# The first layer norm of a hybrid decoder block: ScalarE normalises, scale and bias move to the transposed tiles, and the residual is finished during the up-projection

## The chip, the cores and the metric

One core of a Trainium2 chip runs the whole block as one program. Its engines have queues of their own: TensorE (PE in the profile; PEld is its weight load), VectorE (DVE), ScalarE (ACT), GpSimd (POOL), and SyncE (SP), whose queue here issues all the DMAs that matter. The metric is the device time of one execution in microseconds (us), the median of several.

## The reference, cut to what matters

One layer, 1024 tokens, width 1024, all float32. The change touches the first norm, and what reads its result: the up-projection, and the residual of the second norm.

```python
mixed = (jax.nn.sigmoid(gate_a) * y_a + jax.nn.sigmoid(gate_b) * y_b) @ w_out[i]
x = layer_norm(DEEPNORM_ALPHA * x + mixed, ln1_g[i], ln1_b[i])
h = causal_dwconv(x @ w_up[i], conv_w[i], conv_b[i])          # 1024 -> 5632, 3 taps
h_gate, h_val = jnp.split(h, 2, axis=-1)
ffn = (jax.nn.silu(h_gate) * h_val) @ w_down[i]
x = layer_norm(DEEPNORM_ALPHA * x + ffn, ln2_g[i], ln2_b[i])
...
def layer_norm(x, g, b):                                      # over the last axis
    return (x - mu) * rsqrt(var + 1e-5) * g + b
```

## The kernel before

**Precision.** Each float32 operand of a product is split into a high and a low part in the matmul's own format (`wh`/`wl` for weights): ACT writes the high part (L101), DVE or POOL subtracts it from the source to give the low part (L103, L106). A product is three matmuls, high times high, high times low, low times high (`mm3`, L155).

**Stages.** Input projection, scores and selection, the two token mixers and their projections run until about 1171 us. Then, on which the change bears:

- The out-projection with the first norm, about 1171 to 1302 us (`tm_phase`, L890, called with `FOURS`). The 8 token tiles t = 0 to 7 of 128 tokens go in two groups of four; each group runs over 4 blocks of 256 columns of `w_out`. After each block DVE adds the PSUM to the scaled residual `res` (L965, `mixed`) and takes statistics (L910). When a group's last block is through, `fin1(t)` (L946) follows for each of its tiles, that of group 1 among the matmuls of group 2, that of group 2 (tiles 4 to 7) with no out-projection left behind it. Here this last stretch is called the tail.
- `fin1` runs `layer_norm` (L873), 8 transposes of 128x128 on PE (L88), the copy of the PSUM into `xq` on ACT (L958) and, after each second tile, `x_sets` (L932), which makes the right-hand operands of the up-projection, `XS[0..6]`, by sums on DVE and POOL (L164) and splits (L101, L106). Then SP stores `res` to `d_x1[t]` in HBM (L961).
- `layer_norm`: BN_AGGR on DVE (L876), rsqrt as two small POOL operations (L212, L213), then two DVE passes over 128x1024 (L884: subtract the mean, times the gain; L887: times rsqrt, plus the bias). The gain and bias lie in `gb`, each loaded broadcast to all partitions. Tiles 1 and 3 (`SPREAD`) go another way: one small DVE operation (L879), ACT normalises (L880), DVE multiplies (L881), POOL adds (L882).
- The up-projection, 22 steps f = 0 to 21, about 1294 to 1735 us (`up(f)`, L1006). A step has 7 products p0 to p6 of 12 matmuls with 512 columns (a Winograd-like scheme), 84 matmuls. Its weights come as two raw tiles (`wr` in even steps, `ar` in odd ones) by SP (L995); `left_operands` makes seven weight sets from them by sums on DVE (L164), high parts on ACT, low parts on POOL (DVE in part for f = 0). This chain, DVE, ACT, POOL and again DVE, is called the ring below. DVE gathers the products into `h` (L1020), `conv` runs on ACT (L1062) and DVE (two passes, L1064), ACT makes the silu, POOL the product, and SP stores to `d_act` (L1074).
- The down-projection reads `d_act` back, with `w_down` in `dr` tiles, and `d_x1` as the residual of the second norm (L1183).

**Buffers.** Seven weight sets have seven slots (`wq` 4, `fp` 3): one step's worth. The tag `dr` of pool `raws` holds one buffer at a time. The `ch` PSUM tiles have 8 banks, four in use by a step.

**What sets the order.** The kernel is built with a scheduler that plays a model of the time at build, and writes each engine's queue by it. The place of a line in the code is therefore not its place in the queue; on an engine, instructions run strictly in the order of the queue. Orders shown below are those queues.

## Time and profile before

| | us |
|---|---|
| median of 3 executions (lowest, highest) | 2160.23 (2158.56, 2161.76) |
| the profiled execution | 2157.95 |
| its span in the trace | 2156.2 |
| PE busy in it | 2067.9 |
| DVE busy in it | 1585.9 |

The span runs from the first to the last instruction of the trace, and the remaining 1.75 us lie around it. A row of a timeline has the start, the duration, the engine, the line, the operation, its output and input and the count; a bracket at its end is the idle time of the engine just before it and what ended that. The mean granted TensorE clock is 0.983 of full speed.

### The profile page before, as it was taken

The page shows a single profiled execution, that of the slowest core. Times are in us where ns is not written, and L with a number is a line of the kernel's source. Part 1 is how long each engine was busy: PE and PEld are TensorE (multiplying, and loading weights), DVE is VectorE, ACT ScalarE, POOL GpSimd, SP SyncE. Part 2 cuts the span into 40 slices and gives each one's busy share as a digit, 9 for nine tenths or more (in the row PEclk, how much of TensorE's full clock was granted, in tenths as well). Part 3 has the DMA queues.
Part 4 walks back from the last instruction along what each step waited for, and adds up shares of the span by engine and source line. Part 5 has one row for each costly group of instructions (what it writes and reads, how often), then busy time and mean ns, then how long its engine had stood idle before and what let it go on. Part 6 is the DMA issues. An engine that isn't in the chain of part 4 may idle for free.

```text
span 2156.2 us, 32472 instructions
## 1 busy us (share of the span) xinstructions
PE 2067.9 (96%) x12210; PEld 1815.2 (84%) x12210; DVE 1585.9 (74%) x2700; ACT 841.9 (39%) x1498; POOL 996.8 (46%) x808
## 2 busy tenths in 40 slices
PE   9999999999999999999999979999999978989997
PEld 8888899998988888887788977877777768989897
DVE  3489999999227888786234587777777789986965
ACT  4343312213126766675222244434443444332421
POOL 2432443634431121213332676767767765444743
PEclk9999999999999999999999989999999989999999
DMA  4222211211226776779666351222222134223222
GB/s 137 79 64 79 86 33 55 62 45 52 74 77 126 140 153 133 141 160 227 209 198 148 129 173 49 88 79 78 79 79 88 55 124 150 89 93 118 89 98 79
DMA packets 377566, 227.14 MB, mean 105 GB/s; under 512 B 189328, under 2 KB 351760, under 8 KB 377408
## 3 DMA queue, kind: packets, MB, share of 16 engines
q1 hardware_dynamic: 377408, 225.06, 38.3%
q8 instruction: 96, 1.57, 0.3%
q14 instruction: 62, 0.51, 0.1%
HBM read 146.37 MB, written 40.89 MB: 87 GB/s over the span
## 4 chain that ended last, share of the span: by engine, by line
PE 22%; DVE 12%; POOL 8%; issue 7%; DMA 2%; ACT 2%; SPq 0%; POOLq 0%; DVEq 0%; ACTq 0%
PE mm L155 12%; PE ch L155 10%; POOL wl L106 5%; DVE au L106 2%; DVE cv L1064 1%; DVE wu L106 1%; DVE um L164 1%; DVE h L1020 1%; DVE dr L164 1%; DMA wr<-d_ob 1%; DVE ar L164 1%; ACT cv L1062 1%; DVE res_all L164 1%; POOL lnmv L212 1%; DMA dr<-in_w_down_dram 1%
## 5 line engine op out<-in xcount | busy, mean ns | idle before, releaser
L106 POOL TENSOR_TENSOR wl<-wr,wh 128x512 fp32r<-128x512 f32 x304 | 439.9, 1460 | 287.3 <-ACT wh L101 279.7
L155 PE MATMUL ch<-xs,wh 128*128 128x512 f32 x1232 | 384.8, 394 | 6.7 <-ACT wh L101 4.1
L155 PE MATMUL mm<-Ah,wh 128*128 128x512 f32 x832 | 331.6, 399 | 2.2 <-ACT wh L101 1.3
L155 PE MATMUL mm<-Al,wh 128*128 128x512 f32 x832 | 330.1, 397 | 0.3 <-POOL Al L106 0.3
L155 PE MATMUL mm<-Ah,wl 128*128 128x512 f32 x832 | 329.3, 396 | 0.0
L155 PEld LDWEIGHTS ch<-xs,wh 128*128 128x128 f32 x1232 | 231.7, 189 | 59.4 <-ACT wh L101 4.6
L103 POOL TENSOR_SCALAR wh<-wr 128x512 fp32r<-128x512 f32 x112 | 76.9, 690 | 383.2 <-PE mm L155 199.8
L155 PE MATMUL ch<-xs,wl 128*128 128x512 f32 x616 | 242.4, 394 | 6.6 <-POOL wl L106 6.5
L155 PE MATMUL ch<-wu,au 128*128 128x256 f32 x1512 | 197.1, 294 | 31.2 <-DVE um L164 14.4
L155 PEld LDWEIGHTS ch<-wu,au 128*128 128x128 f32 x1512 | 192.5, 201 | 36.0 <-DVE um L164 14.7
L155 PE MATMUL mm<-wl,Ah 128*128 128x256 f32 x768 | 217.8, 285 | 4.7 <-POOL wl L106 4.6
L155 PE MATMUL mm<-wh,Al 128*128 128x256 f32 x768 | 216.3, 284 | 0.0
L155 PE MATMUL mm<-wh,Ah 128*128 128x256 f32 x768 | 213.8, 284 | 0.0
L1064 DVE SCALAR_TENSOR_TENSOR cv<-h,cw,cv 128x1023 f32<-128x1023 f32 x88 | 167.6, 1905 | 59.9 <-ACT cv L1062 58.4
L101 ACT ACTIVATE wh<-wr 128x512 fp32r<-128x512 f32 (+1 forms) x201 | 120.6, 622 | 186.7 <-PE mm L155 77.0
L155 PEld LDWEIGHTS mm<-Ah,wh 128*128 128x128 f32 x832 | 156.3, 188 | 32.9 <-ACT wh L101 1.8
L155 PEld LDWEIGHTS mm<-Ah,wl 128*128 128x128 f32 x832 | 156.2, 188 | 32.9
L155 PEld LDWEIGHTS mm<-Al,wh 128*128 128x128 f32 x832 | 156.4, 188 | 30.5 <-POOL Al L106 0.8
L651 DVE MATCH_REPLACE8 score<-m,score 128x896 f32<-128x896 f32 (+3 forms) x192 | 166.4, 868 | 0.0
L650 DVE MAX8 m<-score 128x8 f32<-128x896 f32 (+3 forms) x192 | 163.4, 875 | 2.3 <-POOL score L457 2.1
L155 PEld LDWEIGHTS mm<-wl,Ah 128*128 128x128 f32 x768 | 145.8, 190 | 6.4 <-POOL wl L106 5.7
L106 POOL TENSOR_TENSOR wl<-ar,wh 128x512 fp32r<-128x512 f32 x77 | 127.7, 1677 | 44.9 <-ACT wh L101 44.9
(261 smaller groups left out, 4327.0 us busy)
## 6 DMA issues: line engine op xcount, KB each, us to landing
wr<-in_w_in_dram SPq DMA_DIRECT2D x60, 512.0 KB, 3.9
wr<-in_w_up_dram SPq DMA_DIRECT2D x22, 512.0 KB, 3.9
ar<-in_w_up_dram SPq DMA_DIRECT2D x22, 512.0 KB, 3.9
d_act<-cv SPq DMA_DIRECT2D x22, 512.0 KB, 2.6
dr<-in_w_down_dram SPq DMA_DIRECT2D x12, 768.0 KB, 7.1
ar<-d_act SPq DMA_DIRECT2D x12, 768.0 KB, 5.7
d_tg<-tg SPq DMA_DIRECT2D x32, 256.0 KB, 2.0
wr<-in_w_out_dram SPq DMA_DIRECT2D x16, 512.0 KB, 3.6
```

What stands on the lines that cost most here:

```text
L101: S.activation(dst, src, AF.Copy, scale=scale)
L103: (V if eng == "V" else G).tensor_scalar(dst, src, scale, 0.0, ALU.mult, ALU.add)
L106: done["GV"[eng != "G"]] = (G if eng == "G" else V).tensor_tensor(out=dst, in0=src, in1=hi.bitcast(F32), op=ALU.subtract)
L155: T.matmul(ps, lhsT=l, rhs=r, start=start, stop=stop, skip_group_check=more)
L164: (G if eng == "G" else V).tensor_tensor(out=out, in0=a, in1=b, op=op)
L212: G.tensor_scalar(dst, src, scale, eps, ALU.mult, ALU.add)
L650: V.max(m8, score[t])
L651: V.match_replace(score[t], m8, score[t], TAKEN)
L1020: V.tensor_tensor(out=out, in0=a, in1=quad(b), op=ALU.add)
L1062: S.activation(o, h, AF.Identity, bias=cbias[:, c:c + 1], scale=cw[:, 2, c:c + 1])
L1064: V.scalar_tensor_tensor(o[:, d:], h[:, :L - d], cw[:, 2 - d, c:c + 1], o[:, d:], ALU.mult, ALU.add)
```

## The change

`plain_norm` replaces `layer_norm` in `fin1`: ACT normalises each tile in two halves of 512 columns without gain and bias, with a small DVE operation (L877 of the changed kernel) for its bias pointer. Gain and bias are applied after the transposes, where they lie along the partitions: each of the 8 transposed pieces of 128x128 of a tile is read out of PSUM with its own scale and bias column, four by ACT (L974) and four by DVE (L972), in place of two ACT copies of 128x512. The columns come by two small loads into `gb1`. The broadcast loads of gain and bias leave the out-projection. The rows stored are those without gain and bias, to a new `d_n1` (L977). `finish_x1(t)` loads them again into the one buffer `X1`, multiplies by the gain and adds the bias on DVE (two operations of 128x1024, L164 with the name `x1w`), and stores `d_x1` (L1102); it is called after steps f = 4 to 11. `X1` has the tag `dr`, so `w_down`'s first load comes after it. The `SPREAD` path goes. The seven weight slots are dealt differently: sets 0 and 5 lie in an early pool, 1 to 4 in `wq`, 6 in `fp`.

```diff
--- before.py
+++ after.py
@@ -249,6 +249,7 @@
     d_oa = [dp.tile([P, L], F32, name=f"d_oa{j}") for j in range(8)]
     d_ob = [dp.tile([P, L], F32, name=f"d_ob{j}") for j in range(8)]
     d_x1 = [dp.tile([P, D], F32, name=f"d_x1{t}") for t in range(NT)]
+    d_n1 = [dp.tile([P, D], F32, name=f"d_n1{t}") for t in range(NT)]
     d_act = [dp.tile([P, 6, L], F32, name=f"d_act{c}") for c in range(4)]
     d_ma = [dp.tile([P, L], F32, name=f"d_ma{j}") for j in range(8)]
 
@@ -867,8 +868,16 @@
             nc.sync.dma_start(cw[:, i], conv_w[0, i].rearrange("(f p) -> p f", p=P))
         nc.sync.dma_start(cbias, conv_b[0].rearrange("(f p) -> p f", p=P))
 
-    def load_gb(pl, g, b):
-        return [bcast_row(pl, vec[0], D, nm("gb")) for vec in (g, b)]
+    def plain_norm(t, nseg, eps):
+
+        r = RS["res"][t]
+        mv = RS["pool"].tile([P, 4], F32, name=nm("lnmv"), tag="lnmv", bufs=2)
+        V.bn_aggr(mv[:, 0:2], RS["stats"][t][:, :nseg])
+        rsqrt_of(mv[:, 2:3], mv[:, 1:2], 1.0, eps, 1)
+        V.scalar_tensor_tensor(mv[:, 3:4], mv[:, 0:1], -1.0, mv[:, 2:3], ALU.mult, ALU.mult)
+        for h in range(2):
+            c = slice(h * HALF, (h + 1) * HALF)
+            S.activation(r[:, c], r[:, c], AF.Identity, bias=mv[:, 3:4], scale=mv[:, 2:3])
 
     def layer_norm(t, nseg, gb, eps, spread=False, cuts=1):
         r = RS["res"][t]
@@ -922,12 +931,15 @@
     segx = ExitStack()
     segd, segk = ExitStack(), ExitStack()
     xpool = pool("xset", stack=segx)
+    fp0 = pool("ffearly", stack=segx)
+    gb1 = fp0.tile([P, 2, KT], F32, name="gb1")
+    for i, v in enumerate((ln1_g, ln1_b)):
+        nc.sync.dma_start(gb1[:, i], v[0].rearrange("(k p) -> p k", p=P))
     open_residual([x[t * P:(t + 1) * P, :] for t in range(NT)], 5)
     XS = [bpool.tile([P, 2, 4, HALF], F32R, name=nm("xs"), tag="B") for _ in range(4)]
     with ExitStack() as c1:
         lp = pool("ln1", stack=c1)
-        gb1 = load_gb(lp, ln1_g, ln1_b)
-        SPREAD, XE, XA = (1, 3), ('GVGVGVG', 'GVGVGVG', 'GGGVGGG', 'VVGVVGV'), ('VVVV', 'VVVV', 'VVVV', 'VVVG')
+        XE, XA = ('GVGVGVG', 'GVGVGVG', 'GGGVGGG', 'VVGVVGV'), ('VVVV', 'VVVV', 'VVVV', 'VVVG')
 
         def x_sets(i, xf):
 
@@ -944,9 +956,8 @@
         xfs = {}
 
         def fin1(t, nseg):
-            layer_norm(t, nseg, gb1, EPS, t in SPREAD)
+            plain_norm(t, nseg, EPS)
             r = RS["res"][t]
-            tap(f"x1_{t}", r)
             xf = xfs.setdefault(t // 2, [])
             for g in range(2):
                 pt = bank("mm" if t >= 4 else "pt", (P, 4, P))
@@ -955,10 +966,15 @@
                 for k in range(4):
                     n = g * 4 + k
                     turn_tile(pt[:, k], r[:, n * P:(n + 1) * P])
-                S.activation(quad(xq), pt, AF.Copy)
+                for k in range(4):
+                    n, c = g * 4 + k, slice(k * P, (k + 1) * P)
+                    if k % 2:
+                        V.tensor_scalar(xq[:, c], pt[:, k], gb1[:, 0, n:n + 1], gb1[:, 1, n:n + 1], ALU.mult, ALU.add)
+                    else:
+                        S.activation(xq[:, c], pt[:, k], AF.Identity, bias=gb1[:, 1, n:n + 1], scale=gb1[:, 0, n:n + 1])
             if t % 2:
                 x_sets(t // 2, xf)
-            nc.sync.dma_start(d_x1[t], r)
+            nc.sync.dma_start(d_n1[t], r)
 
         def mixed(ps, rvs, *_):
             for j, rv in enumerate(rvs):
@@ -997,7 +1013,7 @@
             for _ in range(7):
                 n = nset[0] % 7
                 nset[0] += 1
-                pl, nb = (wq, 4) if n < 4 else (fp, 3)
+                pl, nb = ((fp0, 2), (wq, 4), (wq, 4), (wq, 4), (wq, 4), (fp0, 2), (fp, 1))[n]
                 W.append([pl.tile([P, 512], F32R, name=nm(x), tag=x, bufs=nb) for x in ("wh", "wl")])
             run(left_operands(raw[1][:, :512], raw[1][:, 512:], raw[0][:, :512], raw[0][:, 512:],
                               lambda j, src: split(*W[j], src, "A", (UE if f else UE0)[j]), US))
@@ -1074,11 +1090,24 @@
                 nc.sync.dma_start(d_act[f // 6][:, f % 6], out_[0])
             return p0, p1, p5, p2, p3, p4, conv1, p6, conv0
 
+        X1 = rawp.tile([P, 3, D], F32, name="x1w", tag="dr")
+
+        def finish_x1(t):
+            nc.sync.dma_start(X1[:, 0], d_n1[t])
+            if t == 0:
+                for i, v in enumerate((ln1_g, ln1_b)):
+                    nc.sync.dma_start(X1[:, 1 + i], v[0].unsqueeze(0).to_broadcast([P, D]))
+            for i, op in enumerate((ALU.mult, ALU.add)):
+                sums(X1[:, 0], X1[:, 0], X1[:, 1 + i], op)
+            nc.sync.dma_start(d_x1[t], X1[:, 0])
+
         late = []
         for f in range(NF):
             p0, p1, p5, p2, p3, p4, conv1, *rest = up(f)
             run([p0, p1, *late[:1], p5, *late[1:], p2, p3, p4, conv1])
             late = rest
+            if 4 <= f < 4 + NT:
+                finish_x1(f - 4)
         late[0]()
         last_conv = late[1]
     segx.close()
```

What the built queues hold, at three places. First DVE in the tail, where the last out-projection blocks of tiles 4 to 7 end (`res` the residual tiles, `mm` PSUM, `lnmv` mean and variance, `wl`/`wh`/`wr` weights of step 0). Before:

```order
L965 SCALAR_TENSOR_TENSOR res_12260<-res_12260,mm_12824 128x256
L876 BN_AGGR lnmv_12905<-stats_12254 128x2
L910 BN_STATS stats_12255<-res_12260 128x6
L884 SCALAR_TENSOR_TENSOR res_12258<-res_12258,lnmv_12905,gb_11734 128x1024
L876 BN_AGGR lnmv_12926<-stats_12255 128x2
L965 SCALAR_TENSOR_TENSOR res_12262<-res_12262,mm_12851 128x256
L887 SCALAR_TENSOR_TENSOR res_12258<-res_12258,lnmv_12905,gb_11736 128x1024
L884 SCALAR_TENSOR_TENSOR res_12260<-res_12260,lnmv_12926,gb_11734 128x1024
L106 TENSOR_TENSOR wl_13047<-wr_13044,wh_13046 128x512
```

After:

```order
L981 SCALAR_TENSOR_TENSOR res_12268<-res_12268,mm_12831 128x256
L919 BN_STATS stats_12264<-res_12268 128x6
L106 TENSOR_TENSOR wl_13110<-wr_13107,wh_13109 128x512
L981 SCALAR_TENSOR_TENSOR res_12270<-res_12270,mm_12858 128x256
L875 BN_AGGR lnmv_12939<-stats_12264 128x2
L164 TENSOR_TENSOR wr_13107<-wr_13107,wr_13105 128x512
L919 BN_STATS stats_12265<-res_12270 128x6
L981 SCALAR_TENSOR_TENSOR res_12272<-res_12272,mm_12885 128x256
```

The low part `wl` of a first weight set, and a sum of its raw weights, moved from behind the first three passes of the norm to either side of tile 5's residual; the norm's passes are gone from this queue.

Second, DVE around the end of `x_sets` and step 0 of the up-projection (`xs` the operands that p0 to p6 read, `h` the gathered products). Before:

```order
L106 TENSOR_TENSOR xs_11730<-xq_12993,xs_11730 128x4x128
L164 TENSOR_TENSOR wr_13042<-wr_13042,wr_13044 128x512
L106 TENSOR_TENSOR xs_11728<-xq_13000,xs_11728 128x4x128
L164 TENSOR_TENSOR wr_13044<-wr_13044,wr_13042 128x512
L106 TENSOR_TENSOR wl_13049<-wr_13042,wh_13048 128x512
L106 TENSOR_TENSOR wl_13053<-wr_13044,wh_13052 128x512
L106 TENSOR_TENSOR wl_13059<-wr_13044,wh_13058 128x512
L1020 TENSOR_TENSOR h_13091<-h_13092,ch_13094 128x4x128
L164 TENSOR_TENSOR ar_13168<-ar_13168,ar_13166 128x512
L164 TENSOR_TENSOR ar_13166<-ar_13166 128x512
L164 TENSOR_TENSOR ar_13166<-ar_13166,ar_13168 128x512
L1020 TENSOR_TENSOR h_13092<-h_13092,ch_13094 128x4x128
```

After:

```order
L164 TENSOR_TENSOR x1w<-x1w 128x1024
L164 TENSOR_TENSOR xq_13059<-xq_13059,xq_13021 128x512
L106 TENSOR_TENSOR xs_11744<-xq_13049,xs_11744 128x4x128
L106 TENSOR_TENSOR xs_11742<-xq_13059,xs_11742 128x4x128
L164 TENSOR_TENSOR ar_13231<-ar_13231,ar_13229 128x512
L164 TENSOR_TENSOR ar_13229<-ar_13229 128x512
L1036 TENSOR_TENSOR h_13154<-h_13155,ch_13157 128x4x128
L164 TENSOR_TENSOR x1w<-x1w 128x1024 x2
L164 TENSOR_TENSOR ar_13229<-ar_13229,ar_13231 128x512
L164 TENSOR_TENSOR x1w<-x1w 128x1024
L1036 TENSOR_TENSOR h_13155<-h_13155,ch_13157 128x4x128
L164 TENSOR_TENSOR x1w<-x1w 128x1024
```

The last `xs` operation now stands behind four `x1w` operations (rows of tiles 0 and 1, the last of them shown first here); weight low parts that followed it have gone ahead; and tiles 2 and 3 stand among step 0's gathers. The remaining `x1w` operations follow in steps 1 to 3, two for each tile.

Third, SP from the loads of step 1's weights on (`d_n` the rows without gain and bias, `d_x` the finished ones, their numbers one per tile). Before:

```order
L961 DMA d_x_141<-res_12258 128x1024
L995 DMA ar_13168<-in_w_up_dram 128x8x128
L995 DMA ar_13454<-in_w_up_dram 128x8x128
L1117 DMA dr_16222<-in_w_down_dram 128x6x256 x2
L961 DMA d_x_142<-res_12260 128x1024
L961 DMA d_x_143<-res_12262 128x1024
L961 DMA d_x_144<-res_12264 128x1024
L995 DMA wr_13310<-in_w_up_dram 128x8x128
```

After:

```order
L977 DMA d_n_149<-res_12268 128x1024
L1096 DMA x1w<-d_n_145 128x1024
L1099 DMA x1w<-in_ln_g_dram 128x1024
L1099 DMA x1w<-in_ln_b_dram 128x1024
L977 DMA d_n_150<-res_12270 128x1024
L1011 DMA wr_13373<-in_w_up_dram 128x8x128
L977 DMA d_n_151<-res_12272 128x1024
L977 DMA d_n_152<-res_12274 128x1024
L1102 DMA d_x_137<-x1w 128x1024
L1096 DMA x1w<-d_n_146 128x1024
L1011 DMA wr_13375<-in_w_up_dram 128x8x128
L1102 DMA d_x_138<-x1w 128x1024
```

The store of each tile's rows is followed by reloads into `x1w` one after another, each behind the store of the tile ahead of it; `w_down`'s loads (`dr`) left this place and stand behind the last of these.

On SP also, five of the loads of `x` into `res` stand some 65 instructions earlier, at what was about 1036 us in the trace of before, in place of 1174.5 us.

## Rows read from the trace of the kernel before

**Rows 1.** The page: busy time and share of the span, by engine.
```profile
PE 2067.9 (96%) x12210; PEld 1815.2 (84%) x12210; DVE 1585.9 (74%) x2700; ACT 841.9 (39%) x1498; POOL 996.8 (46%) x808
```

**Rows 2.** Table by stretches: us, busy time (x count) of each engine, granted clock, DMA share.
```profile
1230.00:1240.00 10.00, 6.88 (x48) 6.66 (x47) 9.63 (x10) 4.39 (x7) 10.00 (x6) 0.83 0.44 171
1290.00:1300.00 10.00, 5.66 (x18) 4.01 (x16) 9.79 (x10) 6.35 (x12) 7.71 (x5) 0.65 0.12 48
```

**Rows 3.** PE timeline in the out-projection: start, us, operation, idle before and releaser.
```profile
1219.39 0.39 PE L155 MATMUL mm<-wl,Ah 128*128 128x256 f32 x1 [1.23 <-POOL wl L106]
...
1235.92 0.58 PE L155 MATMUL mm<-wl,Ah 128*128 128x256 f32 x1 [3.12 <-POOL wl L106]
```

**Rows 4.** POOL timeline, same stretch.
```profile
1228.08 3.11 POOL L882 TENSOR_TENSOR res<-res,gb 128x1024 f32<-128x1024 f32 x1
```

**Rows 5.** The table by stretches: the tail, and steps 0 to 3.
```profile
1269.30:1302.30 33.00, 15.38 (x86) 12.89 (x85) 32.73 (x39) 14.24 (x26) 23.90 (x17) 0.71 0.54 176
1308.50:1368.10 59.60, 59.60 (x264) 49.36 (x263) 41.16 (x38) 24.15 (x35) 37.87 (x23) 1.00 0.20 62
```

**Rows 6.** DVE by form, the tail: us, mean ns, idle before.
```profile
L887 DVE SCALAR_TENSOR_TENSOR res<-res,lnmv,gb 128x1024 f32<-128x1024 f32 x4 | 6.1, 1528 | 0.0
L884 DVE SCALAR_TENSOR_TENSOR res<-res,lnmv,gb 128x1024 f32<-128x1024 f32 x4 | 6.1, 1526 | 0.0
L106 DVE TENSOR_TENSOR wl<-wr,wh 128x512 fp32r<-128x512 f32 x4 | 3.3, 820 | 0.5 <-ACT wh L101 0.5
...
L965 DVE SCALAR_TENSOR_TENSOR res<-res,mm 128x256 f32<-128x256 f32 x4 | 1.6, 397 | 1.8 <-PE mm L155 1.8
```

**Rows 7.** DVE by form, the whole out-projection.
```profile
L887 DVE SCALAR_TENSOR_TENSOR res<-res,lnmv,gb 128x1024 f32<-128x1024 f32 x6 | 9.7, 1612 | 2.0 <-POOL lnmv L213 2.0
...
L879 DVE SCALAR_TENSOR_TENSOR lnmv<-lnmv 128x1 f32<-128x1 f32 x2 | 3.5, 1734 | 0.0
```

**Rows 8.** The gains and biases: duration min/median/max.
```profile
L884 DVE SCALAR_TENSOR_TENSOR res<-res,lnmv,gb x6: 1268/1275/2287, 1215.9 to 1283.9; 128x1024 f32<-128x1024 f32 x6
...
L881 DVE TENSOR_TENSOR res<-res,gb x2: 2235/2276/2318, 1224.3 to 1232.5; 128x1024 f32<-128x1024 f32 x2
```

**Rows 9.** ACT timeline: the wait for the first weights of step 0.
```profile
1272.25 0.63 ACT L101 ACTIVATE wh<-wr 128x512 fp32r<-128x512 f32 x1 [7.20 <-DMA wr<-in_w_up_dram]
```

**Rows 10.** PE timeline in the tail, to the start of p1.
```profile
1274.10 1.03 PE L88 MATMUL mm<-ident,res 128*128 128x128 f32 x8
...
1284.07 1.97 PE L88 MATMUL mm<-ident,res 128*128 128x128 f32 x8 [5.37 <-DVE res L887]
...
1293.71 1.22 PE L155 MATMUL ch<-xs,wh 128*128 128x512 f32 x2 [2.59 <-DVE xq L164]
...
1302.39 1.22 PE L155 MATMUL ch<-xs,wh 128*128 128x512 f32 x2 [4.13 <-ACT wh L101]
```

**Rows 11.** DVE by form, steps 0 to 4.
```profile
L1064 DVE SCALAR_TENSOR_TENSOR cv<-h,cw,cv 128x1022 f32<-128x1022 f32 x7 | 15.3, 2193 | 0.3
L1020 DVE TENSOR_TENSOR h<-h,ch 128x512 f32<-128x512 f32 x20 | 13.4, 683 | 1.6 <-PE ch L155 1.2
L1064 DVE SCALAR_TENSOR_TENSOR cv<-h,cw,cv 128x1023 f32<-128x1023 f32 x7 | 12.1, 1733 | 9.5 <-ACT cv L1062 9.5
```

**Rows 12.** The page: DMAs of 512 KB, median us to landing.
```profile
wr<-in_w_up_dram SPq DMA_DIRECT2D x22, 512.0 KB, 3.9
...
d_act<-cv SPq DMA_DIRECT2D x22, 512.0 KB, 2.6
```

**Rows 13.** PE waits of steps 4 to 21.
```profile
PE ch L155 <- POOL wl L106: 6.5, 16, 0.7
```

**Rows 14.** DVE timeline in a later step: one form, twice.
```profile
1464.59 1.76 DVE L164 TENSOR_TENSOR wr<-wr,wr 128x512 f32<-128x512 f32 x1 [2.43 <-POOL wl L106]
1466.27 0.68 DVE L164 TENSOR_TENSOR ar<-ar,ar 128x512 f32<-128x512 f32 x1
```

**Rows 15.** POOL timeline beside it.
```profile
1464.52 1.28 POOL L106 TENSOR_TENSOR wl<-ar,wh 128x512 fp32r<-128x512 f32 x1
```

## The prediction

> **What bounds the kernel now.** Read the page first: PE is busy 96% of the span [rows 1], so a time can only change where PE waits, or where its granted clock falls. The change touches three stretches, and each has another limit. In the out-projection with group 1's norm PE waits twice for a low part of `w_out` that POOL makes [rows 3], while POOL is full [rows 2] and carries out the bias addition of the `SPREAD` tiles [rows 4]. In the tail DVE is the limit: it is busy 32.73 of 33.00 us [rows 5], the transposes wait for its norm passes, and p0 and p1 for operands whose sums it makes [rows 10]. In steps 0 to 3 of the up-projection PE is busy all 59.60 us, and DVE has 59.60 - 41.16 = 18.4 us idle [rows 5]. Later steps have hardly a wait: 16 waits, 6.5 us in all, in some 335 us [rows 13]. So what PE loses in the early steps nothing gives back later.
>
> All sums are made against the profiled execution, 2157.95 us. The median of the runs is 2.28 us above it, and the forecast is carried over to the median by that.
>
> **Part 1, the out-projection.** POOL loses two additions of about 3.1 us [rows 4], and DVE two multiplications of 2.28 us and two passes each for tiles 0 and 2 [rows 8]; ACT gains the norms there, and is free for more than half of the slice (4.39 of 10.00 us busy [rows 2]). PE's waits of 3.12 and 1.23 us are both for POOL [rows 3]; the first of these numbers stands at 1235.92, behind an addition that began at 1228.08 and the low part after it; the other comes before any addition, so that only relief of DVE and POOL together can remove it. The granted clock of that slice is 0.83 [rows 2]: as a mixture of full (2.4 GHz) and half (1.2 GHz) speed that is 0.34 of 10 us at half speed, or 1.7 us of work lost, and with the wait gone it should stay up, since PE ran without a break before. Lower bound 3.1 (the long wait alone), upper bound 3.12 + 1.23 + 1.7 = 6.1. I take the long wait and its clock, 4.8, or about **-5**.
>
> **Part 2, the tail.** DVE is full here, so its operations are counted one by one, up to the last `xs` operation, on which p1 hangs:
> - Removed: eight norm passes, 4 x 1.526 + 4 x 1.528 = 12.2 us [rows 6].
> - Added: 16 readings of a 128x128 piece out of PSUM. No row has this form; the PSUM readings of 128x256 take 0.397 [rows 6] and of 128x512 0.683 [rows 11], and the line through both gives 0.254 at 128 columns: 16 x 0.254 = 4.1, and 16 x 0.397 = 6.4 at the dear end.
> - Added: four small operations for ACT's bias pointer. Their like took 1.73 [rows 7], more than a whole 128x256 operation with 0.397, so most of that was waiting. I take 0.4 each, 1.6; the dear end is 6.9.
> - Moved ahead of the last `xs`: three low parts (0.82 each [rows 6]) and one sum (1.0, as the mean of its kind beside POOL, an estimate between the 0.68 and the 1.76 of rows 14), 3.5.
> - Moved in: four `x1w` operations of tiles 0 and 1. Two-input operations of 128x1024 took 1.27 at best, 2.28 beside POOL [rows 8], 1.53 in the mean of this very stretch [rows 6]. I take the mean, 6.1, with ends 5.1 and 9.1.
>
> The sum is -12.2 + 4.1 + 1.6 + 3.5 + 6.1 = +3.1 (ends +2 and +13.7). Two waits come on top. The first low part of step 0 now stands ahead of tile 5's residual; the high part that it reads ran on ACT at 1272.25 for 0.63, when the weights had landed [rows 9], and DVE gets there at about 1270.1, one residual and one statistic into the window of rows 5 (some 0.4 us each). It waits 2.8 us, and behind it are queued the residuals and statistics of tiles 5 to 7, so ACT's norms, the transposes, and all that follows. Before, the first norm passes filled that time. The second is the rsqrt on POOL: DVE waited 2.0 us for it in two places [rows 7]; its operations are still there, now with ACT behind them; other DVE work stands in between, so I take 1. ACT's own load grows by eight half norms and loses eight copies of the same size, and splits its copies; at 14.24 of 33.00 us [rows 5] it has room. Total **+7**; ends +2 (no wait) and +18.5 (all dear ends, both waits in full). While PE waits there its clock is down anyway (0.65 between 1290 and 1300 [rows 2]), so nothing more is lost by that.
>
> **Part 3, steps 0 to 3.** The twelve `x1w` operations of tiles 2 to 7 stand there, not in steps 4 to 11. Nearest in size and place are the convolution's two-input passes of 128x1022 and 128x1023, 2.19 and 1.73 [rows 11], mean 1.96: 12 x 1.96 = 23.5 against 18.4 us of idle time, 5.1 too many. The ends are 12 x 1.27 = 15.2, which fits, and 12 x 2.28 = 27.4, 9.0 too many. The idle time isn't wholly free either: 9.5 us of it is the convolution waiting for ACT [rows 11]. The one buffer adds a wait. A tile's rows are loaded only after the tile ahead has been stored: 2.6 + 3.9 = 6.5 us by the nearest transfers [rows 12]. Between tile 2's addition and tile 3's multiplication stands a single sum, so DVE stops some 5.5 us; queued behind are `h` gathers, and the sums of the next weight set. With slots for one step's sets, late sums become late low parts, and PE stops. I count half of that wait (the other half falls on time in which DVE would have waited anyway), 2.8. Together **+8**; ends 0 and 9.0 + 5.5 = +14.5.
>
> **What costs nothing.** The five loads of `x` (2.5 MB) now stand about 140 us earlier, among the loads of the mixers' projections; I take 0, since the stores and loads there have time to spare, with up to +4 if they delay a load that PE waits for. The broadcast loads that left that region speak for 0. `w_down` and the finished rows are first read by the down-projection, after 1735 us; a few swaps in the down-projection are worth 2 us either way. Steps 4 to 21 have the same order as before.
>
> Sum: -5 + 7 + 8 = +10; 2157.95 + 10 + 2.28 = **2170 us**.
>
> **The rivals.**
> - *It fits.* The `x1w` operations run at 1.27 and lie in idle time, the reload wait hits nothing, and the tail costs 5 by its cheaper end and the first wait. Then -5 + 5 + 0 = 0: 2160. For it: 15.2 is under 18.4. Against it: no two-input operation of that size beside a busy POOL averaged 1.27. Chance 0.20.
> - *The shorter tail counts (faster).* Tiles 0 and 1 are finished in gaps that the wait for the rsqrt and the transposes leaves on DVE, the weights land in time, and steps 0 to 3 take up the rest. The tail then gives 12.2 - 4.1 - 1.6 - 3.5 = 3.0, part 1 gives 5: -8, 2152. It decides at p1: it must start before its out-projection's end plus 28.3 us (1302.39 - 1274.10, the latter being where the transposes behind the last out-projection matmul start [rows 10]). For it: 12.2 us leave the engine that is full. Against: 15.3 come in. Chance 0.18.
> - *The shared port.* Of two operations of one form and size one took 1.76, beginning while a POOL subtraction ran, and the next 0.68, with POOL idle [rows 14, 15]. If each of the 16 `x1w` operations meets POOL so, they take 2.28: 4 x 0.75 + 12 x 0.32 = 6.8 more than in the sum, 2177. POOL is busy 23.90 of 33.00 and 37.87 of 59.60 us [rows 5], so about two in three should meet it, not all. Chance 0.08. The Trainium skill says of this (SBUF — State Buffer, section "SBUF: two separate sides") that VectorE and GpSimd share a port pair which is an exclusive lock, held for a whole instruction, against a VectorE operation with two SBUF inputs. By that rule the trace agrees with 1.76 against 0.68; it speaks against the place more than the kind: the passes removed also had two inputs in SBUF, but twelve of the 16 that come in now stand among the ring's POOL operations.
> - *The early loads of x.* They hold up SP and the loads that the mixers wait for, 6 us more: 2176. Chance 0.08; it would show as new PE waits between 1030 and 1090.
>
> **How the numbers follow.** My forecast has 0.46, its own range 2165 to 2182. A measurement of this kernel can tell about 0.2%, 4.3 us, from no change, so faster is under 2155.9 and slower over 2164.5. Slower: 0.46 + 0.08 + 0.08 = 0.62; same 0.20; faster 0.18. The range from 2153 to 2182 leaves out most of the faster rival (0.12) and the top ends of parts 2 and 3 (0.07).
>
> **What would show it.** Part 1: no wait of PE for POOL near 1235.9, and granted clock 1.00 there. Part 2: DVE idle at the first `wl` ahead of tile 5's residual; p1 starting about 35 us behind the last out-projection matmul in place of 28.3. Part 3: `x1w` rows of 1.5 to 2.3 us, one of them behind a DMA wait of some 5 us, PE waits for POOL in steps 1 to 3, and stores to `d_act` further apart than later ones. It is wrong if p1 starts no later against the out-projection's end, or if PE has no new waits in steps 0 to 4.

## The result and the profile after

The changed kernel takes 2170.95 us (median of 4, 2168.8 to 2173.09), the kernel before 2159.39 (2157.45 to 2161.76, with one run more than above): a ratio of 1.0054, 95% interval 1.0041 to 1.0067. That is 11.6 us slower; 2170 was forecast. The profiled execution of after took 2171.09 us with a span of 2169.3, 13.1 more than the span of before, at the same granted clock of 0.983.

Where the 13.1 us lie is read from seven marks in each trace: the first and the last matmul of the out-projection (PE timeline, `mm<-wh,Ah` and its kind), the first gather `h<-h,ch` of p1 (DVE timeline), the first, fourth and last store `d_act<-cv` (SP timeline), and the end of the span. All kernels of this document were cut at the same marks; the differences of the marks are, in us:

| kernel | start to first out-projection matmul | to the last | to the gather of p1 | to the first store | to the fourth | to the last | to the end |
|---|---|---|---|---|---|---|---|
| before | 1171.5 | 102.5 | 34.5 | 29.8 | 59.7 | 369.9 | 388.4 |
| **after** | 1172.5 | **96.7** | **39.3** | **36.9** | **63.6** | 370.2 | 390.2 |
| e1_late | 1173.1 | 97.5 | 35.4 | 29.7 | 59.8 | 395.1 | 386.8 |
| e2_nofinish | 1176.7 | 97.5 | 37.4 | 29.3 | 59.8 | 370.1 | 389.2 |
| e3_xq8 | 1172.3 | 96.7 | 47.7 | 35.6 | 57.9 | 370.1 | 390.4 |
| e4_b_nospread | 1176.2 | 105.3 | 33.2 | 29.7 | 59.7 | 369.5 | 389.0 |
| e6_gap | 1171.1 | 97.3 | 35.6 | 29.5 | 59.8 | 370.6 | 387.3 |
| e7_mix_gap | 1174.4 | 97.8 | 43.6 | 28.8 | 58.0 | 370.2 | 388.4 |
| e8_mix_now | 1176.9 | 98.8 | 41.8 | 28.5 | 59.7 | 370.2 | 387.1 |
| e9_gap_pool | 1174.2 | 97.4 | 36.5 | 30.0 | 59.8 | 370.1 | 389.3 |
| e10_gap_b | 1172.3 | 97.0 | 35.5 | 29.5 | 59.8 | 385.9 | 388.4 |
| e11_gap_hold | 1172.0 | 96.7 | 35.9 | 28.8 | 59.8 | 370.1 | 387.3 |
| e12_gap_again | 1174.5 | 97.2 | 35.4 | 29.5 | 59.8 | 370.5 | 388.6 |
| e12_hold_again | 1173.7 | 97.7 | 35.8 | 28.8 | 59.8 | 370.1 | 386.7 |

The first and the last column vary by some 6 and 4 us between kernels whose code there is alike, and runs of one kernel spread as much; so of after against before they say nothing (+1.0 and +1.8). The rest is clear: -5.8 in the out-projection, +4.7 from its end to the gather of p1, +7.1 and +3.9 from there to the stores of steps 0 and 3.

PE's waits in the changed kernel, 1000 to 1420 us (time in all, how often, the longest), answer to [rows 3, 10]:

```profile
PE ch L155 <- DVE xq L972: 14.0, 1, 14.0
PE mm L88 <- ACT res L880: 6.1, 3, 3.5
PE ch L155 <- DVE h L1036: 5.2, 3, 2.5
PE ch L155 <- POOL wl L106: 1.8, 1, 1.8
...
PE mm L155 <- POOL wl L106: 1.0, 2, 0.8
```

The waits for POOL in the out-projection (3.12 and 1.23 us in [rows 3]) are gone, and the slice that had a granted clock of 0.83 [rows 2] is full. The transposes wait less (6.1 against 11.0 us, the rows of [rows 10] and their like), but p0 now waits 14.0 us, and new waits stand further on, at 1355 to 1390 us, where PE is in steps 2 to 4, ahead of the stores. The table by stretches, with columns as in [rows 2]: the slice of [rows 2], the tail from the last out-projection matmul to the gather of p1, and from there to the fourth store and, within it, to the first:

```profile
1230.00:1240.00 10.00, 10.00 (x88) 10.00 (x87) 7.68 (x15) 6.46 (x14) 6.67 (x6) 1.00 0.79 289
1269.16:1308.44 39.28, 16.61 (x61) 12.45 (x60) 35.26 (x57) 23.26 (x45) 21.79 (x20) 0.65 0.63 214
1308.44:1408.89 100.45, 93.44 (x396) 74.91 (x395) 79.36 (x69) 37.92 (x54) 59.55 (x34) 0.98 0.39 131
1308.44:1345.33 36.89, 36.89 (x162) 30.12 (x161) 27.80 (x26) 14.38 (x21) 19.20 (x12) 1.00 0.34 114
```

and the same of the kernel before, without the first:

```profile
1273.98:1308.52 34.54, 16.83 (x64) 12.78 (x63) 32.22 (x33) 16.72 (x30) 25.97 (x17) 0.65 0.53 170
1308.52:1397.94 89.42, 89.42 (x396) 74.06 (x395) 63.09 (x59) 37.78 (x54) 57.52 (x34) 1.00 0.23 70
1308.52:1338.27 29.75, 29.75 (x133) 24.64 (x132) 19.35 (x20) 12.94 (x18) 15.16 (x10) 1.00 0.18 51
```

In the tail DVE is busy 35.26 us in place of 32.22, so 3.0 of the 4.7 us are work and 1.7 idle time. In the steps PE, which had been busy throughout, is idle for 7.0 us. The other 4.0 of the 11.0 us are longer busy time over the same 396 matmuls (93.44 against 89.42): the granted clock of 0.98 accounts for about 2.0 of them (0.02 of 100.45), the rest isn't settled. The +7.1 up to the first store is no loss of PE's yet: it is busy throughout, and has gone through 162 matmuls in place of 133; only the store comes later in the order. What PE loses lies between the first and the fourth store.

### The profile page after: what moved, and what is told of

Its sections match the earlier page's. It is cut to its first block, busy times and chain, and to the rows that moved or that the text cites. A ratio compares the mean times of both kernels' runs of the same rounds, so it can differ in the third digit from the quotient of the medians.

```text
span 2169.3 us, 32583 instructions
## 1 busy us (share of the span) xinstructions
PE 2072.9 (96%) x12210; PEld 1813.6 (84%) x12210; DVE 1603.9 (74%) x2740; ACT 855.0 (39%) x1528; POOL 983.5 (45%) x806
## 3 DMA queue, kind: packets, MB, share of 16 engines
q1 hardware_dynamic: 381792, 233.46, 39.3%
## 4 chain that ended last, share of the span: by engine, by line
PE 21%; DVE 11%; POOL 8%; issue 6%; DMA 4%; ACT 3%; SPq 0%; POOLq 0%; DVEq 0%; ACTq 0%
PE mm L155 12%; PE ch L155 9%; POOL wl L106 5%; DVE cv L1080 2%; DVE au L106 1%; DVE wu L106 1%; DMA wr<-d_ob 1%; DVE h L1036 1%; ACT cv L1078 1%; DVE um L164 1%; DVE ar L164 1%; DVE res_all L164 1%; DMA ar<-d_act 1%; POOL au L106 1%; DVE dr L164 1%
## 5 line engine op out<-in xcount | busy, mean ns | idle before, releaser
L1080 DVE SCALAR_TENSOR_TENSOR cv<-h,cw,cv 128x1023 f32<-128x1023 f32 x88 | 163.1, 1853 | 53.6 <-ACT cv L1078 52.3
L155 PEld LDWEIGHTS ch<-xs,wl 128*128 128x128 f32 x616 | 116.8, 190 | 39.3 <-POOL wl L106 13.5
```

The source lines that it names most:

```text
L155: T.matmul(ps, lhsT=l, rhs=r, start=start, stop=stop, skip_group_check=more)
L1080: V.scalar_tensor_tensor(o[:, d:], h[:, :L - d], cw[:, 2 - d, c:c + 1], o[:, d:], ALU.mult, ALU.add)
```

## The experiments

Three questions: what finishing costs and why (it is 11 us in steps that had 18.4 us of idle DVE time), what the tail consists of, and what made the out-projection shorter.

### Finishing: where, and whether at all

**e1_late** puts it into the steps that the code names.

```diff
         def finish_x1(t):
-            nc.sync.dma_start(X1[:, 0], d_n1[t])
...
+            with tc.issue_after(kept[0].ins):        # the last store to d_act
+                nc.sync.dma_start(X1[:, 0], d_n1[t])
...
```

> The changed kernel with one edit: on SP, each load of a tile's rows for finishing stands behind the store of the convolution's product of the step before, so that the 16 x1w operations really stand in steps 4 to 11, two per step. Theory (finishing costs because twelve of its operations meet steps 0 to 3, in which DVE has too little room, and four lie in the tail): the loss of 11 us between p1 of step 0 and the steady state goes away, and p1 comes 3 us earlier for the four operations that leave the tail. In steps 4 to 11 DVE has some 5 us idle per step and two operations take 2.5 to 4.5, so the spacing of the d_act stores there stays 19.9. Time 2157 (2154 to 2160). Rival (the ring has no room in any step, the work costs the same wherever it stands): spacing 20.5 to 21.5 in steps 4 to 11, time 2166 to 2171.

Measured: 2179.73 us, ratio to the kernel before 1.0092 (1.0079 to 1.0106). The first steps are clean, as the theory had it (29.7 and 59.8 us in the table), but each of the steps 4 to 11 takes 22.95 us in place of 19.9, eight times 3.05. The theory failed. The rival held in kind, though both its numbers were too low: an operation costs 1.5 us there (16 for 24.4), against 0.9 for the twelve in the first steps of the changed kernel (11.0).

**e2_nofinish** leaves finishing out: the second norm's residual is read without the first norm's gain and bias.

```diff
-            if 4 <= f < 4 + NT:
-                finish_x1(f - 4)
...
-                        nc.sync.dma_start(RS["res"][t], d_x1[t])
+                        nc.sync.dma_start(RS["res"][t], d_n1[t])
```

> The changed kernel without finishing: the residual of the second norm is read from the rows without gain and bias, so the gain and the bias of the first norm are left out of that residual (they stay in the up-projection), and all 16 x1w operations with their loads and stores are gone. Theory: the tail keeps its limit (the last readings out of PSUM, which p0 waits for, and the sums behind them), only shorter by the four operations; steps 0 to 3 run like those of the kernel before. p0 starts about 1294, time 2156 (2153 to 2159), that is within 1 us of finishing late. Rival (what costs in steps 0 to 3 is not finishing but the dealt weight slots): the waits of PE between 1350 and 1391 stay, time over 2165.

Measured: 2158.1 us, ratio 0.9995 (0.9986 to 1.0004), the kernel before within the interval. Steps 0 to 3 are those of before (29.3, 59.8), so the weight slots cost nothing there. Finishing is worth 12.8 us (2170.95 - 2158.1) of the changed kernel's time, all of its loss; without it the change is even.

The trace of e1_late shows why DVE's idle time didn't take the work. DVE in one of its late steps (start, duration, operation, idle before and releaser):

```profile
1441.89 4.32 DVE L1080 SCALAR_TENSOR_TENSOR cv<-h,cw,cv 128x1023 f32<-128x1023 f32 x2 [1.31 <-ACT cv L1078]
1446.20 2.25 DVE L164 TENSOR_TENSOR x1w<-x1w 128x1024 f32<-128x1024 f32 x1
1449.64 1.76 DVE L164 TENSOR_TENSOR ar<-ar,ar 128x512 f32<-128x512 f32 x1 [1.19 <-POOL wl L106]
1451.32 1.21 DVE L164 TENSOR_TENSOR x1w<-x1w 128x1024 f32<-128x1024 f32 x1
1452.46 1.76 DVE L164 TENSOR_TENSOR wr<-wr,wr 128x512 f32<-128x512 f32 x1
1454.14 0.68 DVE L1036 TENSOR_TENSOR h<-h,ch 128x512 f32<-128x512 f32 x1
```

and POOL beside it:

```profile
1441.60 8.01 POOL L106 TENSOR_TENSOR wl<-ar,wh 128x512 fp32r<-128x512 f32 x4
```

In a step without finishing, DVE idles 2.43 us for POOL's low part in front of the weight sum (as in [rows 14]) and some 1.3 to 1.4 us for ACT in front of each of the two convolutions. The first `x1w` sits in the 2.43 us, but lasts 2.25, and POOL's four low parts take 8.01 in place of the 7.02 of a step without it; so the sum still waits 1.19 and starts later. The second (1.21) stands right behind that sum, in front of the next sum and of the gather that PE waits for, and the next sum, now meeting POOL, takes 1.76 in place of 0.68. That is 1.0 + 1.2 + 1.1 = 3.3, about the 3.05. The reading that this suggests: sum, high part, low part, matmul and gather are a closed ring, and what is put into it lengthens every turn, idle time elsewhere or not.

**e6_gap** tests that: the same 16 operations, one per step in steps 4 to 19, in the one place where DVE waits for ACT and POOL is idle.

```diff
             S.activation(o, h, AF.Identity, bias=cbias[:, c:c + 1], scale=cw[:, 2, c:c + 1])
+            gate = ExitStack()
+            if i == 0 and pend:
+                with tc.issue_after(kept[1].ins):    # the last gather
+                    x = pend.pop(0)()                # one x1w operation
+                gate.enter_context(tc.issue_after(x.ins))
...
```

> The changed kernel with the 16 x1w operations put in one place of a step each: one operation per step in steps 4 to 19, on DVE behind the gather of p6 and in front of the convolution's passes, where DVE waits 1.40 us for ACT in each step and POOL is idle for part of it. Theory (finishing late cost 3 us per step because its operations stood in the closed ring, DVE sum, ACT high part, POOL low part, PE, gather, and one of them beside a POOL operation; idle time outside the ring is free): an operation takes 1.21, the spacing of the d_act stores is 19.9 to 20.2, time 2157 to 2162. Rival (DVE has no room in a step, each operation costs 1.5 wherever it stands, as 3.05 per two in the run before): spacing 21.4 in 16 steps, time 2177 to 2182.

Measured: 2156.58 us, ratio 0.9988 (0.9979 to 0.9997), and once more beside another run 2157.74, 0.9987 (0.9978 to 0.9996). The gap in a step of the kernel before:

```profile
1470.27 3.52 DVE L1064 SCALAR_TENSOR_TENSOR cv<-h,cw,cv 128x1023 f32<-128x1023 f32 x2 [1.40 <-ACT cv L1062]
```

DVE in one of the steps of e6_gap, and POOL:

```profile
1423.28 1.28 DVE L1036 TENSOR_TENSOR h<-h,ch 128x512 f32<-128x512 f32 x2
1424.47 1.22 DVE L1109 TENSOR_TENSOR x1w<-x1w 128x1024 f32<-128x1024 f32 x1
1425.94 3.52 DVE L1086 SCALAR_TENSOR_TENSOR cv<-h,cw,cv 128x1023 f32<-128x1023 f32 x2 [0.26 <-ACT cv L1078]
```

```profile
1413.21 7.02 POOL L106 TENSOR_TENSOR wl<-wr,wh 128x512 fp32r<-128x512 f32 x4
...
1422.83 1.69 POOL L106 TENSOR_TENSOR wl<-wr,wh 128x512 fp32r<-128x512 f32 x1 [1.35 <-ACT wh L101]
1426.57 1.81 POOL L106 TENSOR_TENSOR wl<-ar,wh 128x512 fp32r<-128x512 f32 x1 [2.04 <-ACT wh L101]
```

The operation takes 1.22, POOL is idle beside it but for its first 0.05 us, the wait for ACT behind it falls from 1.40 to 0.26, and the spacing of the stores stays 19.9. All 16 together cost nothing.

**e10_gap_b** puts them into the other gap of the same kind, where POOL is busy (`if i == 1` in the lines above).

> The run e6_gap with its 16 x1w operations one gap further: behind the three gathers of p3 and in front of the other convolution's passes, where DVE waits 1.31 us for ACT too, but POOL is in the middle of its 2.42 us product. Theory (a gap takes an operation of 1.22 free only where POOL is idle; beside a POOL operation the same operation takes up to 2.25, which the gap doesn't hold): an operation takes 2.0 to 2.3, spacing 20.4 to 21.4 in 16 steps, time 2164 to 2178. Rival (a gap is a gap): 1.22 each, spacing 19.9, time 2156 to 2158.

Measured: 2170.36 us, ratio 1.0047 (1.0034 to 1.006); the spacing is 20.86 in 16 steps, all as the theory had it. DVE in one of them, and POOL:

```profile
1413.87 2.23 DVE L1109 TENSOR_TENSOR x1w<-x1w 128x1024 f32<-128x1024 f32 x1
1416.03 4.52 DVE L1086 SCALAR_TENSOR_TENSOR cv<-h,cw,cv 128x1023 f32<-128x1023 f32 x2
```

```profile
1412.61 2.42 POOL L164 TENSOR_TENSOR cv<-cv,cv 128x1024 f32<-128x1024 f32 x1 [2.38 <-ACT cv L1088]
1414.98 7.96 POOL L106 TENSOR_TENSOR wl<-wr,wh 128x512 fp32r<-128x512 f32 x4
```

The `x1w` operation begins at 1413.87 during POOL's product, which ends at 1415.03, and ends at 1416.10, 1.07 after that; POOL's four low parts then take 7.96 in place of 7.02. All durations of the 16 operations (min/median/max, ns), in e6_gap, in e10_gap_b and in the changed kernel:

```profile
L1109 DVE TENSOR_TENSOR x1w<-x1w x16: 1216/1218/1219, 1384.6 to 1683.2; 128x1024 f32<-128x1024 f32 x16
```

```profile
L1109 DVE TENSOR_TENSOR x1w<-x1w x16: 2216/2225/2235, 1393.0 to 1705.9; 128x1024 f32<-128x1024 f32 x16
```

```profile
L164 DVE TENSOR_TENSOR x1w<-x1w x16: 1211/1226/2843, 1281.4 to 1370.0; 128x1024 f32<-128x1024 f32 x16
```

Nothing differs between the first two but which gap of a step they stand in. In the changed kernel the operations meet POOL at various points, and there the duration isn't one of two: the seven that begin while a POOL operation has 0.6 to 1.8 us to go take 1.69 to 2.84, and each ends 1.08 to 1.09 us after POOL's. So do the 16 of e10_gap_b and seven of the 16 in e1_late; the nine others of the changed kernel, and the nine of e1_late, take 1.21 to 1.23. An operation that meets POOL so lasts until POOL's own operation is over and 1.08 us more, and POOL's next waits for it in turn, about 1.0 us. The Trainium skill's rule (SBUF — State Buffer, section "SBUF: two separate sides"), an exclusive lock on a shared port pair, held for a whole instruction, is what these rows look like.

Between e6_gap and e10_gap_b the place is all that differs. From e1_late to e6_gap two things changed, the place and the number of operations per step, two in the one and one in the other. So that the ring takes nothing is a reading of e1_late's rows, which no run shows by itself.

### The tail

**e3_xq8** gives the transposed tiles eight buffers, with the weight slots as before to make room.

```diff
-                pl, nb = ((fp0, 2), (wq, 4), (wq, 4), (wq, 4), (wq, 4), (fp0, 2), (fp, 1))[n]
+                pl, nb = (wq, 4) if n < 4 else (fp, 3)
...
-                xq = lp.tile([P, HALF], F32, name=nm("xq"), tag="xq", bufs=5)
+                xq = lp.tile([P, HALF], F32, name=nm("xq"), tag="xq", bufs=8)
```

> The changed kernel with the weight slots dealt as before (four and three) and, in the room that frees, eight buffers in place of five for the transposed tiles xq; finishing is left as it is in the changed kernel. Theory (p0 waits for PSUM banks that the last readings out of PSUM give back, and those wait for an xq buffer that the sums for tiles 4 and 5 hold): the last reading ends by 1288, p0 starts at 1288 to 1291 in place of 1296.7; p1 gains less, 2 to 4 us, since DVE's sums in front of the last xs operation stay; time 2167 to 2169. Rival (the early slots matter more than xq): p0 later than 1296.7, time 2171 to 2175.

Measured: 2171.61 us, ratio 1.0054 (1.0041 to 1.0068), the changed kernel's own time, which the theory missed. In the changed kernel p0 starts 0.06 us after the last reading out of PSUM:

```profile
1268.18 0.69 DVE L106 TENSOR_TENSOR wl<-wr,wh 128x512 fp32r<-128x512 f32 x1 [2.54 <-ACT wh L101]
...
1281.35 1.23 DVE L164 TENSOR_TENSOR x1w<-x1w 128x1024 f32<-128x1024 f32 x1 [0.34 <-DMA x1w<-in_ln_g_dram]
...
1296.27 0.40 DVE L972 TENSOR_SCALAR xq<-mm,gb 128x128 f32<-128x128 f32 x1
1296.60 2.25 DVE L164 TENSOR_TENSOR x1w<-x1w 128x1024 f32<-128x1024 f32 x1
```

```profile
1296.73 1.22 PE L155 MATMUL ch<-xs,wh 128*128 128x512 f32 x2 [14.04 <-DVE xq L972]
...
1302.51 0.49 PE L155 MATMUL ch<-xs,wh 128*128 128x512 f32 x1 [1.09 <-ACT xs L101]
```

With eight buffers p0 starts 17.2 us after the last out-projection matmul in place of 27.6, as the theory has it for readings that wait for a buffer. But that gains nothing: PE then waits for an operand's high part, and the gather of p1 comes 8.4 us later. Its waits in the tail:

```profile
PE ch L155 <- DVE xq L972: 9.9, 1, 9.9
PE ch L155 <- ACT xs L101: 8.1, 2, 6.5
```

Slots and buffers changed together here, so which of them moved p0, and which delayed p1, isn't told apart.

**e9_gap_pool** takes e6_gap and gives POOL four more of step 0's low parts (`UE0 = 'VGGGGGG'` for `'VVGVVGV'`).

> The run e6_gap with one edit in the tail: of step 0's seven weight sets POOL makes six low parts in place of two, so that DVE has four subtractions fewer in front of the last xs operation. Theory (p1 starts when DVE's queue in the tail is through): from the last out-projection matmul to the gather of p1 33 to 34.5 us in place of 35.6, time 2154 to 2156. Rival (POOL's subtractions hold up DVE's two-input operations beside them, or come late themselves): 35.5 to 37 us, time 2156 to 2159.

Measured: 2158.65 us, ratio 0.9991 (0.9983 to 1.0), the tail 36.5 us. The rival held: four operations fewer on DVE shorten nothing.

**e11_gap_hold** takes e6_gap and holds DVE's part of those weight sets back behind tile 7's residual.

```diff
-            run(left_operands(...))
+            with ExitStack() if f else tc.issue_after(RS["last"].ins):   # tile 7's residual
+                run(left_operands(...))
```

> The run e6_gap with one edit in the tail: DVE's part of step 0's weight sets stands behind the residual of tile 7, so that DVE doesn't wait for the first high part (2.8 us in that run) in front of the residuals and statistics of tiles 5 to 7. Theory (that wait is a term of the tail, since the norms of three tiles are queued behind it): the wait goes, from the last out-projection matmul to the gather of p1 33 to 34 us in place of 35.6, time 2154 to 2156. Rival (the tail is set by the sums and readings behind it, and the subtractions only move into it): 35.5 to 38 us, time 2156 to 2159.

Measured: 2152.22 us, ratio 0.9975 (0.9962 to 0.9988). The theory's time, but not by its mechanism: the wait for the first high part is gone from DVE's waits, and the tail is 35.9 us, no shorter. So the rival is right on the tail, and the gain lies elsewhere. To see whether there is one, both kernels ran again on one chip.

> The kernel of the run e6_gap once more, beside the next one on one chip, since the medians of e6_gap and e11_gap_hold (2156.6 and 2152.2) come from different chips and their traces are alike stage by stage. Theory (the hold in the tail changes nothing; what differed is the spread of the early part): both medians within 2 us of each other, both 0.1 to 0.3% under the kernel before. Rival (the hold is worth 4 us): this one 2155 to 2158, the other 3 us or more below.

> The kernel of the run e11_gap_hold once more, beside the run e12_gap_again on one chip. Theory: within 2 us of that run. Rival: 3 us or more below it, 2151 to 2154.

Measured: 2157.74 and 2153.91 us, ratios 0.9987 (0.9978 to 0.9996) and 0.9975 (0.9965 to 0.9985). The rival held, and the 4 us are real. From the last out-projection matmul to the end, the two traces of each kernel give 882.8 and 883.9 without, 882.0 and 881.2 with the hold, so 1.8 us in the mean lie there. The traced executions differ by no more than that as a whole, since e6_gap's (2152.91 us) lies 3.7 under that run's median, so the traces can't show where the other half is. Of the 1.8 us, 0.7 lie between the gather of p1 and the first store in both pairs; the rest, mostly in the down-projection, whose order on the engines the hold changed as well, is no more than the traces of one kernel differ by. Which of the moved instructions brings the gain stays open. This kernel is the fastest here: 0.25% under the kernel before, and 0.8% under the changed one.

### The out-projection

**e4_b_nospread** is the kernel before without POOL's additions: `SPREAD = ()` for `(1, 3)`.

> The kernel before with one edit: tiles 1 and 3 are normalised like the others (two DVE passes), so the bias addition on POOL is gone and DVE keeps its load. Theory (PE's wait of 3.12 us at 1235.9 comes from the POOL additions in front of the weights' low parts): that wait and the dip of the clock behind it go, out-projection shorter by 3 to 5 us, time 2155 to 2157. Rival (POOL is late because it shares time with DVE's two-input passes, whoever adds): the wait stays within 1 us of itself, time 2159 to 2161.

Measured: 2163.44 us, ratio 1.0016 (1.0007 to 1.0024). Neither range of time was met. The out-projection is 105.3 us, 2.8 more than before, and PE's waits for POOL stay. In this run, and then in the kernel before:

```profile
PE mm L155 <- POOL wl L106: 5.3, 4, 2.1
PE mm L155 <- ACT wh L101: 1.6, 1, 1.6
```

```profile
PE mm L155 <- POOL wl L106: 4.6, 3, 3.1
```

So taking the additions away isn't enough; since two more tiles with two DVE passes came in their place, the run doesn't tell whether the additions were a cause.

**e7_mix_gap** sends only tiles 0 to 3 the new way and finishes them as e6_gap does; **e8_mix_now** finishes them at once, in their own buffers.

```diff
-            plain_norm(t, nseg, EPS)
+            if t < 4:
+                plain_norm(t, nseg, EPS)
+            else:
+                layer_norm(t, nseg, gbr, EPS)
...
+            if t < 4:                                # e8_mix_now alone
+                for i, op in enumerate((ALU.mult, ALU.add)):
+                    sums(r, r, gbr[i], op)
```

> Half of the change: tiles 0 to 3 (their norm lies among the out-projection's matmuls) go the new way, tiles 4 to 7 (the tail) the old way with two DVE passes and one ACT copy; weight slots as before; only tiles 0 to 3 are finished later, one operation per step in steps 4 to 11 in the place of the run e6_gap. Theory (the gain of the change is in the out-projection, its losses in the tail and in finishing): from the first to the last out-projection matmul 96.5 to 98 us as in the changed kernel (102.5 before), from there to the gather of p1 33 to 35 us as before (39.3 in the changed kernel), spacing of the d_act stores 19.9 to 20.2. Time 2153 to 2157, faster than both. Rival (the out-projection's gain needs the tail's part too, or the early slots): 101 us or more there, time 2158 to 2162.

> The same half of the change, but tiles 0 to 3 are finished at once, in their own buffers during the out-projection (two DVE operations of 128x1024 each), so there is no reload and nothing in the up-projection. DVE then has the same eight two-input passes there as before, only off the way to the transposes, and POOL's additions are gone. Theory (what POOL is late for is DVE's two-input passes beside it): most of the out-projection's gain goes, 99 to 102 us from its first to its last matmul, time 2156 to 2160. Rival (what counted was that the transposes waited for the passes, and the additions on POOL): 96.5 to 98 us, time 2152 to 2156.

Measured: 2162.62 and 2162.65 us, ratios 1.0014 (1.0006 to 1.0023) and 1.002 (1.0011 to 1.0029). In the out-projection both keep most of the gain: 97.8 and 98.8 us against 96.7 in the changed kernel and 102.5 before; 97.8 is in the theory's range, 98.8 lies between the two ranges given. In e8_mix_now DVE carries out eight passes of 128x1024 there, beside POOL (in the kernel before six, with POOL's two additions), and PE waits little for POOL:

```profile
PE mm L155 <- DVE res L991: 1.4, 1, 1.4
PE mm L155 <- POOL wl L106: 1.2, 3, 0.6
```

So DVE's passes as such bring back no more than 2.1 of the 5.8 us. What all the kernels with 96.7 to 98.8 us share is that ACT normalises tiles 0 to 3, that the transposes wait for no DVE pass, and that POOL adds nothing; these three weren't taken apart. The expectations on the whole time failed at the tail, which was 43.6 and 41.8 us though tiles 4 to 7 went the old way: in e8_mix_now's queue of DVE all five of its low parts of step 0's weights stand ahead of the last `xs` operation, against two in the kernel before. That alone doesn't explain it, since all five stand ahead of it in e6_gap too, whose tail is 35.6 us without norm passes on DVE. Why the old norm's tail is 7 to 9 us longer in these queues than in that of the kernel before stays open.

## Why the prediction came out right, point by point

- **The total.** -5, +7 and +8 were forecast, +10 in all; -5.8, +4.7 and +11.0 were measured, +9.9. That the total fits so well is luck: part 2 was 2.3 too high and part 3 3.0 too low, and part 3 rests on a mechanism that the runs don't bear out. The signs of all three were right.
- **Part 1, -5.** It was -5.8, between the value taken and the upper bound of 6.1: both waits and the dip of the clock went. The cause was put too narrowly: the step ties the long wait to POOL's additions, and e4_b_nospread shows that without them alone the waits stay. That the early loads of `x` cost nothing held within the spread: the nine traces with the early loads reach the out-projection at 1171.1 to 1176.7 us, the five without (the kernel before, e3_xq8, e4_b_nospread, e7_mix_gap, e8_mix_now) at 1171.5 to 1176.9.
- **Part 2, +7.** It was +4.7. DVE by form in the tail of the changed kernel (us, mean ns, idle before), beside [rows 6, 7]:

```profile
L164 DVE TENSOR_TENSOR x1w<-x1w 128x1024 f32<-128x1024 f32 x4 | 5.9, 1476 | 0.3 <-DMA x1w<-in_ln_g_dram 0.3
L972 DVE TENSOR_SCALAR xq<-mm,gb 128x128 f32<-128x128 f32 x16 | 5.7, 400 | 0.0
L106 DVE TENSOR_TENSOR wl<-wr,wh 128x512 fp32r<-128x512 f32 x5 | 3.7, 748 | 2.7 <-ACT wh L101 2.5
...
L877 DVE SCALAR_TENSOR_TENSOR lnmv<-lnmv 128x1 f32<-128x1 f32 x4 | 1.6, 406 | 0.9 <-POOL lnmv L213 0.8
```

  The operations were priced well: 5.9 for the four `x1w` (6.1 said), 1.6 for the small ones (1.6), the subtractions at 0.75 (0.82). The readings out of PSUM took 0.40 each (5.7 in all, since neighbours overlap), the dear end, not 0.254: such a reading of 128 columns costs what the residual's of 256 does, 0.397 [rows 6], so the line through two sizes was wrong by 1.6 in all. The sum of work, +3.1, stands against 3.0 more busy time, so the misses of single terms cancel there. The wait for the first high part came as said (2.54 at 1268.18, in the tail's rows above; 2.8 said), but it is the term that failed: e11_gap_hold takes it away and the tail stays. It also stood ahead of the mark from which the tail is counted here. What the four `x1w` operations cost is told by the runs without them: 39.3 against 35.4 to 35.9 in e1_late, e6_gap, e10_gap_b and e11_gap_hold, some 3.7. e2_nofinish, with 37.4, fits less well; its queue of DVE in the tail differs from e6_gap's in a few places. The rest, +1, is what the new norm costs without finishing, where the sum without `x1w` had -3.0 and 3.8 of waits.
- **What bounds the tail.** "DVE is the limit" held for the kernel before only in so far as it was busy; e9_gap_pool takes work away from it without gain, and without the `x1w` operations, in e6_gap, it is busy 28.84 of 35.59 us. The prediction hung p1 on the last `xs` operation and had no term for p0. In e1_late, e2_nofinish, e6_gap and e9_gap_pool PE has no wait from the start of p0 to the gather of p1, and p0 starts about 0.05 us after DVE's last reading out of PSUM; in e6_gap:

```profile
1294.97 0.40 DVE L972 TENSOR_SCALAR xq<-mm,gb 128x128 f32<-128x128 f32 x1
```

```profile
1295.43 1.22 PE L155 MATMUL ch<-xs,wh 128*128 128x512 f32 x2 [13.24 <-DVE xq L972]
```

  So there the end of the tail follows that reading. It is over 26.9 us after the last out-projection matmul in e6_gap, 27.8 in e9_gap_pool and 26.5 in e11_gap_hold: neither edit brings it forward by more than 0.4 us. Which chain through DVE, ACT, POOL and the buffers makes it late isn't settled; e6_gap with eight `xq` buffers wasn't run.
- **Part 3, +8.** It was +11.0, with ends 0 and +14.5. The mechanism that carried the sum was wrong in kind: work was set against idle time, and only what exceeded 18.4 us was counted. The measured work was less (12 operations of 1.73 in the mean, 20.8 in place of 23.5), and the waits for the one buffer were short (3.2 us in three places, not 5.5 in one), so the sum with measured prices would have been 2.4 + 1.6 = 4. A term for the granted clock, 0.98 in these steps, was missing too. What the runs show in its place: what an operation costs hangs on where in a step it stands, not on how much idle time DVE has. In e1_late 16 operations cost 8 x 3.05 = 24 us, in e10_gap_b 16 x 0.96 = 15, in e6_gap none; between the last two by place alone.
- **The rivals.** "It fits" is what e6_gap does, at 1.22 an operation (1.27 was supposed), but not where the scheduler put them. "The shared port" was given as 2.28 for each operation; in the changed kernel the median is 1.23 and the highest 2.84, and nine of the 16 weren't held up by a POOL operation. Its mechanism was real, and e10_gap_b shows its price. "The shorter tail" and "the early loads" didn't come.
- **The signs named.** The wait near 1235.9 and the dip are gone; DVE idles at the first low part; PE has new waits in steps 2 to 4, three for gathers (5.2 us) and one for POOL (1.8), where waits for POOL in steps 1 to 3 were named; the stores stand 23.2 and 20.5 us apart, then 19.9. p1 starts 33.4 us behind the last out-projection matmul (the row at 1302.51 above), where some 35 was named, and DVE's waits for the reload are 3.2 us in all, where one of some 5 was named.

## What to carry to other kernels

Before moving work into an engine's idle time, ask what each idle stretch waits for: here a stretch inside a closed chain with the limiting engine seems to have had no room, while one that waits for a third engine took an operation shorter than itself for nothing, as long as POOL stood idle beside it. Place such work by an explicit edge, since a scheduler that plays a time model may put it anywhere, even into steps ahead of those the code names; then read its place in the built queue. And price a move by its neighbours: here the same operation cost 0, 1 or 1.5 us per piece by what stood beside it and behind it.

## What the runs showed of the hardware

A sum or product of two SBUF tiles of 128x1024 on DVE takes 1.21 to 1.23 us when no POOL operation holds it up. Begun while one has at least 0.6 us to go, it ends 1.08 to 1.09 us after that one (30 of 30 in the changed kernel, e1_late and e10_gap_b), and POOL's next low parts take about 1.0 us longer. It can go the other way: in e3_xq8 a low part that POOL began during a DVE sum took 5.21 us. It ended 1.1 us after the last of eight DVE operations on SBUF tiles that followed one another without a gap from 1286.06 to 1291.49.

```profile
1287.40 5.21 POOL L106 TENSOR_TENSOR wl<-wr,wh 128x512 fp32r<-128x512 f32 x1 [4.18 <-ACT wh L101]
```

A VectorE reading of 128x128 out of PSUM with scale and bias by pointer takes 0.40 us, as long as a residual's of 128x256 [rows 6].
